# Feed-forward input products by Strassen's seven block products over token halves, with the weight sums on GpSimd

## The chip, the cores and the metric

The kernel runs on one core of a Trainium2 chip. The time is the device time of one execution in microseconds (us); the profile comes from one profiled execution and its span is counted from the first to the last instruction. The engines are named as in the profile: PE is TensorE (matmul), PEld its weight loads, DVE is VectorE, ACT is ScalarE, POOL is GpSimd, SP is the engine whose queue issues the loads.

## The reference: two decoder layers, of which the feed-forward part matters here

The program is a decoder trunk of two layers on 512 tokens of 1024 features, batch 1, all in float32. Each layer has a mixing half (a gated linear recurrence beside latent attention, merged and projected) and a feed-forward half. The change is in the second:

```
h = rms_norm(x) * (1 + sc_f) + sh_f                 # 512 x 1024
gate, up = jnp.split(h @ w_ffn_in, 2, axis=-1)      # w_ffn_in: 1024 x 5632, gate and up 512 x 2816
x = x + g_f * ((jax.nn.silu(gate) * up) @ w_ffn_out)
```

The six vectors `sh_m .. g_f` of a layer come from `c @ w_ada + b_ada`, a product of one row with a 1024 x 6144 matrix for each layer ("modulation").

## The kernel before

**Layout and precision.** Activations lie feature-major: a tile is 128 features by 512 tokens. To keep float32 accuracy every operand is split in two numbers of a type that the matmul takes at full rate (float32r): ScalarE copies the operand into the high part, VectorE subtracts it from the operand for the low part (`split`). A product takes three matmuls (`mm3`): high x high, high weights x low activations, low weights x high activations. A block of 128 output features is 8 feature tiles x 3 = 24 matmuls of 512 columns into one PSUM tile.

**Feed-forward stage.** `layer` makes `fh`, `fl` (high and low parts of the 8 tiles of h), once per layer, from x, the scale and shift columns and the broadcast `rs`, the reciprocal root of the statistics. While these are late, `Ahead.units` multiplies gate and up tile 0 with x times the scale, and the result is corrected afterwards; part of that correction runs on GpSimd. Then `gemm_units` runs over the other 21 pairs of gate and up tiles: `w_cols` loads 1024 x 128 weights (512 KB) into a `raw` buffer (three of them, `NRAW`) and splits them into `whi` and `wlo` (three of each, `NHL`); 24 matmuls; `done_fi` takes the Silu of a gate tile on ScalarE, multiplies it with the up tile on VectorE and splits the result into `ah`, `al`. The 22 activation tiles come in two halves: after tiles 0 to 10 the first half of the output product is added to the residual (8 units of 33 matmuls), after tiles 11 to 21 the second.

**Background.** After each unit `bg` issues a step of the modulation of the next layer (in layer 0's feed-forward stage, seven segments of nine steps): a load of 512 KB into `graw` (two buffers) and two VectorE operations that add it, times a column, to `macc`. `drain_bg` issues what is left before the second output product. The loads of a step are not issued before the last matmul that stood in the program at that point.

**Order.** The body only records its calls. `Recorder.order` lists them by a greedy schedule with estimated durations: each engine takes, of the calls that are ready and whose tiles have a free buffer, the one with the longest remaining path, with the matmuls chained in program order for that path. In this order each engine's queue is then written, and the engines run their queues in order. GpSimd and VectorE have durations of their own in this schedule; nothing in it lets one slow the other down. All recorded calls are issued from one line of the program, so nearly every row of the profile says L503 and is told apart by its tile names.

**Buffers.** 72 units of 128 x 512 float32 (`NU`) hold all activations and small weights; PSUM has 8 tiles of 128 x 512.

Of the kernel before, what the change touches and what calls it, by code (L numbers as in the profile page):

```python
# [13 lines left out]
F32R = mybir.dt.float32r  # L14
# [7 lines left out]
P = 128  # L22
# [3 lines left out]
KD = D // P  # L26
# [43 lines left out]
NHL = 3  # L70
# [24 lines left out]
# The body below records its engine calls in program order. order() then lists them by a  # L95
# simulated greedy schedule: each engine takes, of the calls whose operands are ready and whose
# tiles have a free buffer, the one with the longest remaining path. The calls are issued in
# that order, and Tile puts in the waits that the data needs.
# [22 lines left out]
class Ref:  # L121
    """A view of a tile that is made when the first call on it is issued."""

    def __init__(self, root, steps, dtype, part, free, off):
        self.root, self.steps, self.dtype = root, steps, dtype
        self.part, self.free, self.off = part, free, off  # (start, count), [(stride, count)], column
# [67 lines left out]
class Recorder:  # L194
# [107 lines left out]
    def order(self):  # L302
# [8 lines left out]
        # longest remaining path, with the products chained in program order  # L311
# [14 lines left out]
        # users of each tile  # L326
# [12 lines left out]
        def fits(o):  # L339
            """a free buffer for each new tile, and one more for each tile that the program makes before it"""  # L340
# [17 lines left out]
        # the clock of the tensor engine: full speed after a window full of work, half after an idle one  # L358
# [31 lines left out]
        def fill():  # L390
            """keeps the clock of the idle tensor engine up until the first products are through"""
            o = ops[self.fill] if self.fill is not None else None
            if o is None or self.fill not in issued or self.fill_end in issued or now < FILL_FROM or fills[0] >= FILL_MAX:
                return
            fills[0] += 1
            busy["PE"] = True
            res.append(o)
            heapq.heappush(events, (now + clock(now, o.dur, True), next(seq), "free", "PE"))
# [119 lines left out]
def trunk(  # L518
# [43 lines left out]
    def mm2(ps, wboth, xh, xl, start, stop):  # L562
        """high and low parts of 64 columns at once: their products lie in the two halves of the partitions"""
# [3 lines left out]
    def mm3(ps, wh, wl, xh, xl, start, stop):  # L567
        T.matmul(ps, wh, xh, start=start, stop=False)
        T.matmul(ps, wh, xl, start=False, stop=False)
        T.matmul(ps, wl, xh, start=False, stop=stop)  # L570

# [1 line left out]
    def raw_tile():  # L573
        return rec.tile(wp, [P, 1024], F32, "raw", NRAW, nm("raw"))

    def hl_tiles():
        return (
            rec.tile(wp, [P, 1024], F32R, "whi", NHL, nm("whi")),
            rec.tile(wp, [P, 1024], F32R, "wlo", NHL, nm("wlo")),
        )  # L580
# [9 lines left out]
    def w_cols(src, nk=KD, on_g=False, raws=None):  # L590
        """src: rows (k p), 128 columns; gives [(hi, lo)] over k, and adds the blocks as loaded to raws"""
# [12 lines left out]
    def w_krope(l):  # L604
        """rotary key columns: high and low parts side by side"""
# [12 lines left out]
    def w_first(l, j, keep):  # L618
        """rows of feature tile j: columns of x_lru tiles 0 and 1 and of all the down projections; gives the
        five (hi, lo), the rotary key columns' high and low parts side by side, and the columns as loaded"""  # L620
# [23 lines left out]
    def w_lru(l, n0):  # L644
        """input and recurrence gate weights of blocks n0..n0+3"""
# [8 lines left out]
    def w_rope(l, g):  # L654
        """rotary query weights of heads 4g..4g+3, as [k][half][head, 32]"""
# [16 lines left out]
    def w_pair(l, p2):  # L672
        """query (no rotary) and key/value weights of heads 2*p2, 2*p2+1"""
# [49 lines left out]
    mods = {}  # L723

    def mod_steps(l, s):
        """generator: one segment (1024 columns) of c @ w_ada[l] + b_ada[l], as columns [128, 8]"""
# [25 lines left out]
    def mod_products(l, s):  # L752
        """the same segment on the tensor engine: w_ada stationary, c moving"""
# [21 lines left out]
    # ---- work for the tensor engine while it waits at the start, so that its clock stays up  # L775
# [32 lines left out]
    def rsqrt(r, ssum, n, w, eps):  # L808
        """r = (ssum / n + EPS) ** -0.5: the reciprocal of what the Sqrt table gives, and one Newton step"""
# [11 lines left out]
    def sqrt_eps():  # L821
        """EPS as a column by the Sqrt table, not before the last call so far: the table is there
        when the statistics are"""
# [6 lines left out]
    class Stat:  # L830
# [13 lines left out]
        def finish(self, cs, n, sbuf=False):  # L844
            """rstd broadcast over partitions, in columns cs of PSUM or of a tile in SBUF"""
# [26 lines left out]
    # Across a norm the products go on before its statistics are there: the first units take x times  # L872
    # the scale, and their results are multiplied by rstd and get the shift's share as a column.
    class Ahead:
# [12 lines left out]
        def units(self, srcs):  # L887
            """products with the column blocks srcs: PSUM tiles, and the shift's columns"""
# [21 lines left out]
    def gemm_units(units, xh, xl, get_w, done):  # L910
        """units: (m, column slice); weights of m by get_w(m): list over k of (hi, lo) APs"""
# [34 lines left out]
    # The first products run by feature tile, each as soon as its modulation is there: scale and  # L946
    # shift of a few tiles at a time come from the columns of w_ada that they take.
    def first_mods(j0, nj, engs):
        """scale or shift, or both, of feature tiles j0 .. j0 + nj - 1"""
# [40 lines left out]
    def first_products(hh, hl):  # L990
# [26 lines left out]
        # Where the shift comes late, the products take the scaled tile without it, and their  # L1017
        # share of the shift is added as a column per accumulator.
# [39 lines left out]
    def tables():  # L1058
# [11 lines left out]
        # positions: rope tables and reset row  # L1070
# [16 lines left out]
        # scol = -8 softplus(-a_param), log1p(u) = 2 atanh(u / (2 + u))  # L1087
# [18 lines left out]
    def small_norm(src, gcol, n):  # L1106
        """src: list of f32 tiles; returns hi/lo tiles of rms-normed src with gain"""
# [12 lines left out]
    def layer(l, rs, ahead):  # L1120
# [13 lines left out]
        # -- down projections  # L1134
# [41 lines left out]
        # -- recurrent branch: projection, convolution, gates  # L1176
# [62 lines left out]
        # -- attention with the branch gates  # L1239
# [63 lines left out]
        def scores(h):  # L1303
            """softmax numerators and their normalisation: P[t] of [128 queries, (t + 1) * 128 keys]"""
# [23 lines left out]
        def transposes(pr):  # L1328
            """P transposed, hi and lo: per key tile, [128 keys, queries from that tile on]"""
# [36 lines left out]
        def merge(h):  # L1366
            """twice y: sigmoid(g) = (1 + tanh(g / 2)) / 2, and the half goes into the scale of the residual"""
# [18 lines left out]
        # -- output projection, residual, statistics of the next norm  # L1386
# [19 lines left out]
        # -- feed-forward  # L1406
        fh = [unit("fh", F32R) for _ in range(KD)]
        fl = [unit("fl", F32R) for _ in range(KD)]
        rs = st.finish(FULL, D, sbuf=True)
        (pg, pu), (cg, cu) = ahead.units([w_fi[l, :, c0 : c0 + P] for c0 in (0, D_FF)])  # L1410
        make_h(l, SH_F, SC_F, fh, fl, rs, FULL)
# [137 lines left out]
```

## Time and profile before

| | |
|---|---|
| median of 3 runs | 1367.09 us (1364.15 to 1371.42) |
| profiled execution, span from first to last instruction | 1361.9 us |
| busy: TensorE, VectorE, ScalarE, GpSimd | 98%, 64%, 46%, 16% |
| feed-forward stage of layer 0 | 346.67 to 700.82 us |
| feed-forward stage of layer 1 | 1000.16 to 1343.86 us |

The profiled execution's own time is its span; what lies around the span in a timed run is the 5.2 us by which the median stands above it. A timeline row has the start, the duration, the engine, and the tile written, `<-`, the tiles read; in brackets the idle time before it and what ended it. Durations of neighbours in a queue overlap by some tens of ns on VectorE and by more on TensorE, so costs in a full queue are taken from start to start.

### The profile page before, as it was taken

How to read it: one execution, taken by the hardware profiler on the slowest of the kernel's cores; microseconds unless marked ns; L12 is line 12 of the kernel's file. 1: busy time of each engine (PE TensorE's matmuls, PEld its weight loads, DVE VectorE, ACT ScalarE, POOL GpSimd, SP SyncE). 2: the span in 40 equal slices, each digit the busy share in tenths (PEclk: the TensorE clock that was granted, in tenths of full speed). 3: DMA queues.
4: the chain of work that ended last, by engine and by line, in shares of the span. 5: the costliest groups of instructions: out<-in, count | busy, mean ns of one | idle time of the engine just before them, and what ended most of it. 6: DMA issues, size and time to landing. Idle time of an engine off the chain costs nothing.

```text
span 1361.9 us, 17108 instructions
## 1 busy us (share of the span) xinstructions
PE 1339.6 (98%) x6330; PEld 1117.8 (82%) x6330; DVE 872.4 (64%) x1478; ACT 623.5 (46%) x963; POOL 213.2 (16%) x238
## 2 busy tenths in 40 slices
PE   8999989999999999999999999999999999999997
PEld 7788878887888888888888888888888888888887
DVE  5898799788856455556869887667673333333344
ACT  5585856644432222322356767855452322232223
POOL 1613334413000000000040243413400000000000
PEclk9999989999999999999999999999999999999999
DMA  9636344334655556555635333311433323433232
GB/s 300 200 96 168 103 124 140 124 117 137 194 182 164 163 159 206 178 170 184 203 86 141 92 86 100 94 47 47 124 89 98 89 75 104 120 93 95 77 88 81
DMA packets 251297, 174.92 MB, mean 128 GB/s; under 512 B 12767, under 2 KB 235341, under 8 KB 251213
## 3 DMA queue, kind: packets, MB, share of 16 engines
q1 hardware_dynamic: 251212, 173.82, 42.3%
q8 instruction: 50, 0.82, 0.2%
q14 instruction: 35, 0.28, 0.1%
HBM read 167.50 MB, written 2.10 MB: 125 GB/s over the span
## 4 chain that ended last, share of the span: by engine, by line
PE 84%; DVE 6%; DMA 5%; issue 2%; POOL 1%; ACT 1%; SPq 1%; ACTq 0%; DVEq 0%; POOLq 0%
PE mm L503 75%; PE s L503 4%; PE o L503 3%; DMA graw<-in_w_ada_dram 2%; PE pt L503 2%; DMA wa<-in_w_ada_dram 2%; DMA raw<-in_w_in_dram 1%; DVE macc L503 1%; DVE ri L503 1%; DVE wlo L503 1%; DVE xc L503 1%; POOL w L503 1%; DVE wacc L503 1%; SPq L503 1%; DVE sc L503 0%
## 5 line engine op out<-in xcount | busy, mean ns | idle before, releaser
L503 ACT ACTIVATE whi<-raw 128x1024 fp32r<-128x1024 f32 (+2 forms) x226 | 219.7, 973 | 581.3 <-PE mm L503 371.1
L503 DVE TENSOR_TENSOR wlo<-raw,whi 128x1024 fp32r<-128x1024 f32 (+2 forms) x218 | 249.3, 1145 | 205.5 <-ACT whi L503 201.2
L503 PE MATMUL mm<-fh,wlo 128*128 128x512 f32 x672 | 261.9, 390 | 0.0
L503 PE MATMUL mm<-fh,whi 128*128 128x512 f32 x672 | 261.7, 389 | 0.0
L503 PE MATMUL mm<-fl,whi 128*128 128x512 f32 x672 | 261.6, 389 | 0.0
L503 PE MATMUL mm<-hh,whi 128*128 128x512 f32 x408 | 161.3, 396 | 0.0
L503 PE MATMUL mm<-hl,whi 128*128 128x512 f32 x408 | 160.2, 393 | 0.0
L503 PE MATMUL mm<-hh,wlo 128*128 128x512 f32 x400 | 156.3, 391 | 0.0
L503 PEld LDWEIGHTS mm<-fl,whi 128*128 128x128 f32 x672 | 126.1, 188 | 26.4 <-DVE fl L503 0.2
L503 PEld LDWEIGHTS mm<-fh,wlo 128*128 128x128 f32 x672 | 126.1, 188 | 26.4 <-DVE wlo L503 0.3
L503 PEld LDWEIGHTS mm<-fh,whi 128*128 128x128 f32 x672 | 126.2, 188 | 26.0
L503 PE MATMUL mm<-ah,whi 128*128 128x512 f32 (+1 forms) x363 | 139.7, 385 | 0.0
L503 PE MATMUL mm<-ah,wlo 128*128 128x512 f32 (+1 forms) x363 | 139.3, 384 | 0.0
L503 PE MATMUL mm<-al,whi 128*128 128x512 f32 (+1 forms) x363 | 139.0, 383 | 0.0
L503 DVE SCALAR_TENSOR_TENSOR macc<-graw,cols,macc 128x512 f32<-128x512 f32 x140 | 103.8, 777 | 24.1 <-DMA graw<-in_w_ada_dram 23.7
L503 DVE TENSOR_TENSOR sg<-sg,mm 128x512 f32<-128x512 f32 x42 | 28.9, 688 | 111.1 <-PE mm L503 111.1
L503 PEld LDWEIGHTS mm<-hl,whi 128*128 128x128 f32 x408 | 77.0, 189 | 15.5 <-DVE hl L503 0.5
L503 PEld LDWEIGHTS mm<-hh,whi 128*128 128x128 f32 x408 | 77.0, 189 | 15.1 <-DVE whi L503 0.2
L503 PEld LDWEIGHTS mm<-hh,wlo 128*128 128x128 f32 x400 | 75.4, 189 | 15.8 <-POOL wlo L503 0.3
L503 PEld LDWEIGHTS mm<-ah,wlo 128*128 128x128 f32 x363 | 68.2, 188 | 13.3
L503 PEld LDWEIGHTS mm<-al,whi 128*128 128x128 f32 x363 | 68.2, 188 | 13.1
L503 PEld LDWEIGHTS mm<-ah,whi 128*128 128x128 f32 x363 | 68.2, 188 | 13.1
(266 smaller groups left out, 2173.9 us busy)
## 6 DMA issues: line engine op xcount, KB each, us to landing
raw<-in_w_ffn_in_dram SPq DMA_DIRECT2D x88, 512.0 KB, 3.9
graw<-in_w_ada_dram SPq DMA_DIRECT2D x80, 512.0 KB, 4.8
raw<-in_w_in_dram SPq DMA_DIRECT2D x49, 512.0 KB, 4.0
raw<-in_w_ffn_out_dram SPq DMA_DIRECT2D x32, 384.0 KB, 3.5
raw<-in_w_ffn_out_dram SPq DMA_DIRECT2D x32, 320.0 KB, 3.2
wa<-in_w_ada_dram SPq DMA_DIRECT2D x32, 256.0 KB, 5.6
raw<-in_w_out_dram SPq DMA_DIRECT2D x16, 512.0 KB, 3.9
raw<-in_w_uq_dram SPq DMA_DIRECT2D x24, 128.0 KB, 3.5
```

Of the source, the lines that this page charges most:

```text
L503: o.call(*(real(v) for v in o.a), **{k: real(v) for k, v in o.k.items()})
```

## The change

Each pair of a gate tile and an up tile of the 21 is now computed as a 2 x 2 block product. The block rows are gate and up, the inner blocks are features 0 to 511 and 512 to 1023, the block columns are tokens 0 to 255 and 256 to 511. Seven products of half the inner size and half the tokens take the place of eight, in the form that uses four sums of weight blocks (S1 to S4) and four of activation blocks (T1 to T4). `token_halves` makes the activation blocks once per layer, `w_quarters` the weight blocks of each pair, `fi_pair` runs the products and puts them together: three PSUM tiles of 256 columns, which take two or three products each, one after the other, and are read in between. The weight buffers `whi` and `wlo` become one kind with six buffers; a pair takes two for A1 and one for A22, and eight units for S1 to S4. Two steps of background follow each pair, as many as before. Comments are taken out elsewhere; the rest of the program is unchanged.

```diff
-NHL = 3
+NHL = 6
...
+    def w_quarters(srcs):
+        raws = []
+        for src in srcs:
+            raw = raw_tile()
+            DMA.dma_start(raw.rearrange("p (k c) -> p k c", c=P), src.rearrange("(k p) c -> p k c", p=P))
+            raws.append(raw)
+        lo_, hi_ = slice(0, 512), slice(512, 1024)
+        a11, a12, a21, a22 = raws[0][:, lo_], raws[0][:, hi_], raws[1][:, lo_], raws[1][:, hi_]
+        s1, s2, s3, s4 = (unit("ws") for _ in range(4))
+        res = {}
+        h, l_ = hl_tiles()
+        split(h, l_, raws[0])
+        res["A11"], res["A12"] = (h[:, lo_], l_[:, lo_]), (h[:, hi_], l_[:, hi_])
+
+        def add(name, s):
+            res[name] = unit("wsh", F32R), unit("wsl", F32R)
+            split(*res[name], s)
+
+        G.tensor_tensor(s1, a21, a22, ALU.add)
+        G.tensor_tensor(s2, s1, a11, ALU.subtract)
+        add("S2", s2)
+        G.tensor_tensor(s3, a11, a21, ALU.subtract)
+        add("S3", s3)
+        add("S1", s1)
+        h = hl_tile("whi")
+        split(h[:, lo_], h[:, hi_], a22)
+        res["A22"] = h[:, lo_], h[:, hi_]
+        G.tensor_tensor(s4, a12, s2, ALU.subtract)
+        add("S4", s4)
+        return res
+
+    def token_halves(first, second):
+        res = {q: [] for q in ("B11", "B21", "B22", "T1", "T2", "T3", "T4")}
+        for a, b in zip(first, second):
+            q = unit("xq", F32R)
+            split(q[:, H0], q[:, H1], a[:, H0])
+            res["B11"].append((q[:, H0], q[:, H1]))
+        t12, t34 = [], []
+        for a, b in zip(first, second):
+            t, u = unit("t12"), unit("t34")
+            V.tensor_tensor(t[:, H0], a[:, H1], a[:, H0], ALU.subtract)
+            V.tensor_tensor(t[:, H1], b[:, H1], t[:, H0], ALU.subtract)
+            G.tensor_tensor(u[:, H0], b[:, H1], a[:, H1], ALU.subtract)
+            G.tensor_tensor(u[:, H1], b[:, H0], t[:, H1], ALU.subtract)
+            t12.append(t)
+            t34.append(u)
+        for src, names in ((t12, ("T1", "T2")), (second, ("B21", "B22")), (t34, ("T3", "T4"))):
+            for t in src:
+                h, l_ = unit("xqh", F32R), unit("xql", F32R)
+                split(h, l_, t)
+                for q, cs in zip(names, (H0, H1)):
+                    res[q].append((h[:, cs], l_[:, cs]))
+        return res
...
-        make_h(l, SH_F, SC_F, fh, fl, rs, FULL)
+        ht = []
+        for j in range(KD):
+            t = unit("ht")
+            V.scalar_tensor_tensor(t, x[j], mcol(l, SC_F, j), rs, ALU.mult, ALU.mult)
+            A.activation(t, t, AF.Identity, bias=mcol(l, SH_F, j))
+            ht.append(t)
+        fx = token_halves(ht[: KD // 2], ht[KD // 2 :])
...
+        def fi_pair(fi):
+            wa = w_quarters([w_fi[l, :, c0 + fi * P : c0 + (fi + 1) * P] for c0 in (0, D_FF)])
+            a, b, z = psum("mm"), psum("mm"), psum("mm")
+            pq, u3, g, t = unit("pq"), unit("u3"), unit("sg"), unit("ut")
+            p1, u2, u3 = pq[:, H0], pq[:, H1], u3[:, H0]
+            a, b, z = a[:, H0], b[:, H0], z[:, H0]
+
+            def product(ps, w, xq, first):
+                n = len(fx[xq])
+                for k, (xh, xl) in enumerate(fx[xq]):
+                    wh, wl = (q[:, k * P : (k + 1) * P] for q in wa[w])
+                    mm3(ps, wh, wl, xh, xl, first and k == 0, k == n - 1, skip_group_check=True)
+
+            product(a, "A11", "B11", True)
+            A.activation(p1, a, AF.Copy)
+            product(b, "S2", "T2", True)
+            V.tensor_tensor(u2, b, p1, ALU.add)
+            product(a, "A12", "B21", False)
+            A.activation(g[:, H0], a, AF.Silu)
+            product(b, "S3", "T3", False)
+            V.tensor_tensor(u3, b, p1, ALU.add)
+            product(z, "S1", "T1", True)
+            V.tensor_tensor(t[:, H1], z, u3, ALU.add)
+            product(b, "A22", "T4", False)
+            V.tensor_tensor(t[:, H0], b, p1, ALU.add)
+            product(z, "S4", "B22", False)
+            V.tensor_tensor(g[:, H1], z, u2, ALU.add)
+            A.activation(g[:, H1], g[:, H1], AF.Silu)
+            V.tensor_tensor(g, g, t, ALU.mult)
+            act_split(fi, g)
+            bg(2)
...
-        gemm_units(
-            [(m, FULL) for m in range(2, 2 * NFH)], fh, fl, w_fi_cols, done_fi,
-        )
+        for fi in range(1, NFH):
+            fi_pair(fi)
```

## Rows read from the trace of the kernel before

**Rows 1.** The page: span, busy time of each engine, and the chain that ended last.
```profile
span 1361.9 us, 17108 instructions
PE 1339.6 (98%) x6330; PEld 1117.8 (82%) x6330; DVE 872.4 (64%) x1478; ACT 623.5 (46%) x963; POOL 213.2 (16%) x238
...
PE 84%; DVE 6%; DMA 5%; issue 2%; POOL 1%; ACT 1%; SPq 1%; ACTq 0%; DVEq 0%; POOLq 0%
```

**Rows 2.** Windows: length, busy us of PE, PEld, DVE, ACT, POOL, clock, DMA.
```profile
150.00:185.00 35.00, 31.74 (x155) 26.15 (x153) 29.45 (x58) 24.75 (x46) 18.65 (x18) 0.98 0.25 77
...
346.67:700.82 354.15, 354.15 (x1570) 292.51 (x1568) 221.37 (x311) 109.11 (x142) 15.27 (x22) 1.00 0.55 176
1000.16:1343.86 343.70, 343.70 (x1529) 284.53 (x1529) 130.05 (x170) 98.39 (x126) 0.00 (x0) 1.00 0.32 92
```

**Rows 3.** Groups by form, PE: count, busy us, mean ns of one.
```profile
L503 PE MATMUL mm<-fh,whi 128*128 128x512 f32 x672 | 261.7, 389 | 0.0
```

**Rows 4.** The chain in order of time: start us, length us, what.
```profile
437.56 57.24 PE mm L503 x252
...
1345.77 2.64 PE mm L503 x22
```

**Rows 5.** Timeline, DVE, from 186 us: start us, length us.
```profile
186.39 0.41 DVE L503 TENSOR_TENSOR pl<-pt,ph 128x256 fp32r<-128x256 f32 x1
186.73 0.68 DVE L503 TENSOR_TENSOR xcl<-xc,xch 128x512 fp32r<-128x512 f32 x1
187.33 0.68 DVE L503 TENSOR_TENSOR kl<-mm,kh 128x512 fp32r<-128x512 f32 x1
187.93 1.40 DVE L503 SCALAR_TENSOR_TENSOR macc<-graw,cols,macc 128x512 f32<-128x512 f32 x2
189.25 0.68 DVE L503 TENSOR_TENSOR ql<-mm,qh 128x512 fp32r<-128x512 f32 x1
```

**Rows 6.** Timeline, DVE, in layer 0's feed-forward stage.
```profile
392.35 1.23 DVE L503 TENSOR_TENSOR wlo<-raw,whi 128x1024 fp32r<-128x1024 f32 x1 [0.16 <-ACT whi L503]
393.49 0.69 DVE L503 TENSOR_TENSOR al<-sg,ah 128x512 fp32r<-128x512 f32 x1
```

**Rows 7.** Groups by form, DVE, 346.67 to 700.82 us.
```profile
L503 DVE SCALAR_TENSOR_TENSOR macc<-graw,cols,macc 128x512 f32<-128x512 f32 x98 | 69.5, 747 | 15.4 <-DMA graw<-in_w_ada_dram 15.1
...
L503 DVE TENSOR_TENSOR al<-sg,ah 128x512 fp32r<-128x512 f32 x22 | 15.1, 685 | 0.0
```

**Rows 8.** POOL: one tile's durations (ns min/median/max), and a group's mean.
```profile
L503 POOL TENSOR_TENSOR ri<-ri,sg x16: 1281/1298/2216, 176.8 to 944.9; 128x512 f32<-128x512 f32 x16
...
L503 POOL TENSOR_TENSOR wsa<-wsa 128x256 f32<-128x256 f32 x6 | 5.2, 879 | 0.2
```

**Rows 9.** Timeline, DVE and POOL, 179 to 182 us.
```profile
176.79 4.36 POOL L503 TENSOR_TENSOR ri<-ri,sg 128x512 f32<-128x512 f32 x2
178.48 1.61 DVE L503 TENSOR_TENSOR_SCAN ri<-a,ri 128x512 f32<-128x512 f32 x1
180.01 0.72 DVE L503 SCALAR_TENSOR_TENSOR xc<-mm,cols,xc 128x510 f32<-128x510 f32 x1
180.65 1.58 DVE L503 TENSOR_TENSOR wlo<-raw,whi 128x1024 fp32r<-128x1024 f32 x1
```

**Rows 10.** Timeline, DVE and POOL, from 338 us.
```profile
336.74 2.52 POOL L503 TENSOR_TENSOR wsa<-wsa,wsb 128x512 f32<-128x512 f32 x2
...
338.09 1.20 DVE L503 TENSOR_TENSOR nt<-nt,ms 128x4 f32<-128x4 f32 x1
```

**Rows 11.** Groups by form, ACT.
```profile
L503 ACT ACTIVATE whi<-raw 128x1024 fp32r<-128x1024 f32 x153 | 162.2, 1060 | 387.8 <-PE mm L503 225.3 <-issue 148.7 <-DMA raw<-in_w_in_dram 9.5
...
L503 ACT ACTIVATE ah<-sg 128x512 fp32r<-128x512 f32 x44 | 27.8, 633 | 1.9 <-DVE sg L503 0.9
```

**Rows 12.** Waits of SP's queue: us in total, times, longest us.
```profile
SPq L503 <- DVE wlo L503: 888.3, 198, 19.3
```

**Rows 13.** DMA issues: count, KB each, median us to landing.
```profile
raw<-in_w_ffn_in_dram SPq DMA_DIRECT2D x88, 512.0 KB, 3.9
```

More of the change, by code (lines that the diff above doesn't have):

```diff
@@ L565, in mm2, with mm3, hl_tile @@
         T.matmul(ps, wboth, xl, start=False, stop=stop)
[L567 to L570, printed above, removed]
+    def mm3(ps, wh, wl, xh, xl, start, stop, **k):
+        T.matmul(ps, wh, xh, start=start, stop=False, **k)
+        T.matmul(ps, wh, xl, start=False, stop=False, **k)
+        T.matmul(ps, wl, xh, start=False, stop=stop, **k)
     def raw_tile():
         return rec.tile(wp, [P, 1024], F32, "raw", NRAW, nm("raw"))
+    def hl_tile(name):
+        return rec.tile(wp, [P, 1024], F32R, "whl", NHL, nm(name))
     def hl_tiles():
-        return (
-            rec.tile(wp, [P, 1024], F32R, "whi", NHL, nm("whi")),
-            rec.tile(wp, [P, 1024], F32R, "wlo", NHL, nm("wlo")),
-        )
+        return hl_tile("whi"), hl_tile("wlo")
     def split_halves(raw, name):
@@ L1404, in layer @@
         )
-        fh = [unit("fh", F32R) for _ in range(KD)]
-        fl = [unit("fl", F32R) for _ in range(KD)]
         rs = st.finish(FULL, D, sbuf=True)
         (pg, pu), (cg, cu) = ahead.units([w_fi[l, :, c0 : c0 + P] for c0 in (0, D_FF)])
-        make_h(l, SH_F, SC_F, fh, fl, rs, FULL)
+        ht = []
[5 more added lines that the diff above has]
+        fx = token_halves(ht[: KD // 2], ht[KD // 2 :])
         if l == 0 and G_F not in EARLY_MODS:
@@ L1415, in layer, with act_split @@
             background.extend(mod_steps(l + 1, s) for s in (SC_M, SH_M, G_M, SC_F, SH_F, G_F))
-        sg, ah, al = {}, {}, {}
+        ah, al = {}, {}
+        def act_split(fi, s):
+            ah[fi], al[fi] = unit("ah", F32R), unit("al", F32R)
+            split(ah[fi], al[fi], s)
         s, t = unit("sg"), unit("ut")
@@ L1421, in layer @@
         V.scalar_tensor_tensor(s, t, cu, s, ALU.add, ALU.mult)
-        ah[0], al[0] = unit("ah", F32R), unit("al", F32R)
-        split(ah[0], al[0], s)
+        act_split(0, s)
         bg(2)
-        def done_fi(m, cs, ps):
-            fi = m // 2
-            if m % 2 == 0:
-                s = unit("sg")
-                A.activation(s[:, cs], ps[:, cs], AF.Silu)
-                sg[fi, cs.start] = s
-            else:
-                s = sg.pop((fi, cs.start))
-                V.tensor_tensor(s[:, cs], s[:, cs], ps[:, cs], ALU.mult)
-                if fi not in ah:
-                    ah[fi], al[fi] = unit("ah", F32R), unit("al", F32R)
-                split(ah[fi][:, cs], al[fi][:, cs], s[:, cs])
-        def w_fi_cols(m):
-            c0 = (m // 2) * P + (m % 2) * D_FF
-            return w_cols(w_fi[l, :, c0 : c0 + P])
+        def fi_pair(fi):
[27 more added lines that the diff above has]
+            bg(2)
         def w_fo_cols(half):
@@ L1505, in done_last @@
                         DMA.dma_start(out[0, t * P : (t + 1) * P, i * 512 : (i + 1) * 512], xo[t][i])
-        gemm_units(
-            [(m, FULL) for m in range(2, 2 * NFH)], fh, fl, w_fi_cols, done_fi,
-        )
+        for fi in range(1, NFH):
+            fi_pair(fi)
         gemm_units(
@@ L1513, in layer @@
         )
-        gemm_units([(m, FULL) for m in range(2 * NFH, 2 * NF)], fh, fl, w_fi_cols, done_fi)
+        for fi in range(NFH, NF):
+            fi_pair(fi)
         drain_bg()
```

## The prediction, made before the changed kernel was run

> **What bounds the kernel now.** I read the page's head first: TensorE is busy 98% of a span of 1361.9 us, VectorE 64%, GpSimd 16%, and the chain that ended last is 84% TensorE, 75% of it the accumulating products `mm` [rows 1]. Then the two feed-forward stretches as windows: 346.67 to 700.82 us (layer 0) and 1000.16 to 1343.86 us (layer 1). In both TensorE is busy all the time at a granted clock of 1.00, VectorE 221 of 354 us and 130 of 344 us, GpSimd 15 us and nothing [rows 2]. So these 698 us are bound by the rate of matmuls, and whatever takes columns away from TensorE is a gain as long as the helpers keep up.
>
> **Matmuls: what is removed.** A matmul's listed 389 ns [rows 3] overlaps its neighbours; the chain gives the rate: 252 products of 512 columns in 57.24 us, 0.2271 us each, and 22 products of 256 columns in 2.64 us, 0.120 us each [rows 4]. One feed-forward pair (gate and up tile) is now 2 x 8 x 3 = 48 products: 10.90 us. After, it is 7 x 4 x 3 = 84 products of 256 columns: 10.08 us. Every product keeps its own weight load; the 22 measured ones had theirs too, so its cost is inside 0.120. There are 21 such pairs in a layer (the first goes through the look-ahead unit, unchanged), 42 in all: 42 x 0.82 = 34.4 us less for TensorE, the most that the change can bring. The Trainium skill (TensorE: Matmul & The Clock Gate, Back-to-back issue gap) counts 262 cycles for 256 columns and 518 for 512; by it a pair would go from 10.4 to 9.2 us and the gain would be 50 us (estimates). The rows have both shapes, and I keep their 34.4.
>
> **VectorE: what is added.** Costs are start to start in a full queue: 256 columns 0.34 us, 512 columns 0.60, an accumulating 512 (`macc`) 0.66 [rows 5], a 1024 weight remainder 1.14 [rows 6]. Per pair before: two weight remainders, the gate product and its remainder: 2 x 1.14 + 2 x 0.60 = 3.48 us. After: one 1024 remainder (A1), four of S1 to S4 and one of A22 (512 each), four sums and one more that read PSUM (u2, u3, two of t, one of g; 256 each), g x t and its remainder: 1.14 + 5 x 0.60 + 5 x 0.34 + 2 x 0.60 = 7.04 us. In layer 0 the background modulation adds two steps per pair of two `macc` operations each: 4 x 0.66 = 2.65 us (98 accumulating ones lie in this stretch now [rows 7]).
>
> **GpSimd: four sums per pair.** A 128x512 tensor_tensor there takes 1.28 us undisturbed and up to 2.2 us [rows 8]. What else it costs stands in two stretches. At 178 us two such operations took 4.36 us instead of 2.57, while VectorE ran scans over two SBUF operands; the weight remainder that VectorE began at 180.65 ended at 182.23, 1.08 us after the GpSimd operation's end at 181.15, about its whole undisturbed time; the `xc` operation between them, which reads PSUM, took its normal 0.72 [rows 9]. At 338.09 a VectorE operation of 4 columns took 1.20 us and ended as the GpSimd operation did [rows 10]. So a GpSimd sum and a VectorE operation with two SBUF operands exclude each other for their whole length. The Trainium skill says the same (SBUF — State Buffer, Who interferes with whom): the shared ports are an exclusive lock, the second to issue blocks fully, and an operation with at most one SBUF input goes free. The trace agrees (the remainder was late by 0.50 us, `xc` not at all); by the rule the sums are not free work beside VectorE.
>
> I take 1.15 us as the hold of one sum (1.07 to 1.26 by [rows 9, 10]): 4 x 1.15 = 4.6 us per pair. Of VectorE's 7.04 us, 5.34 need the same ports; 1.70 read PSUM and can run beside a sum.
>
> **Sum per pair.** Layer 1: VectorE's stream is between 7.04 + 4.6 - 1.70 = 9.9 us (PSUM readers all under sums) and 11.6 us (none). VectorE's queue is in order, so a PSUM reader gets under a sum only if it is at the head then, about a quarter of the time: I take 0.8 us of overlap, 10.8 us. That is above TensorE's 10.08, and the two must also wait for each other. A product is 12 x 0.120 = 1.44 us, and each PSUM tile is read by VectorE between two products that accumulate into it, with one other product as cover: the read itself (0.41 us), the signals, a remainder ahead of it in the queue (0.6 to 1.14 us) and a sum's hold together exceed that often. Behind such a wait TensorE's whole queue stands, and behind VectorE's own waits the next pair's remainders. I take 11.2 us (10.08 at best; 12.5 if three of the waits cost 0.5 us each on top): (11.2 - 10.90) x 21 = +6 us, ends -17 and +34.
>
> Layer 0: the same with 2.65 us of background, which all uses the shared ports. If it stays in the pairs, 13.5 to 14.3 us; the order is made by longest remaining path, which puts background last, so some moves into the 16 output units, where VectorE has room. I take 2.3 us staying and 13.1 us: (13.1 - 10.90) x 21 = +46 us, ends -17 (all moved or hidden) and +71.
>
> **Start of the stage.** After the statistics VectorE needs 16 operations at 0.66 = 10.6 us for fh and fl [rows 5]. After: 8 scaled tiles (5.3), four 256-column remainders (1.4), eight 256-column differences (2.7) and twelve 512 remainders (7.2), 16.6 us, and eight 256-column GpSimd differences, which hold some 0.55 us each (0.88 listed [rows 8]): 21 us. The look-ahead unit covers some 6 us of that in both versions, and the products of A11 and A12 some more. As VectorE bounds what follows, little comes back: +8 us a layer (ends 0 and 10), +16.
>
> **Costed at nothing.** ScalarE: per pair 1.06 + 5 x 0.62 for weights and two conversions, 0.63 for the activation, about 1.1 for one copy and two Silus of half width: 5.9 of 10 us [rows 11]; without room it would add to the remainders' start. Bytes loaded are the same. TensorE's clock: its new waits are each shorter than the ones it now has around 150 to 185 us, where it was busy 31.74 of 35 us and the granted clock was 0.98 [rows 2]. Weight buffers are six of one kind instead of three of two.
>
> **Total.** 6 + 46 + 16 = +68 on a span of 1361.9: 1430. The median of the runs shown is 1367.09, 5.2 us above the span, which I keep: **1435 us**. With all low ends -34 (1333), with all high ends +125 (1492).
>
> **The rivals.**
> *TensorE stays the bound.* The sums find their time, waits vanish: -34 and some +10 at the starts: -24, 1343 us. For it: layer 1 leaves VectorE idle 214 of 344 us now [rows 2]. Against: in layer 0 the shared ports alone need 5.34 + 4.6 + 2.65 = 12.6 us a pair, above 10.08.
> *A split result.* Layer 1 runs at TensorE's pace (-17), layer 0 loses with most background moved out (11.6 us a pair, +15), starts +12: +10, 1377 us (1360 to 1400). It needs near-perfect packing in layer 1.
> *The weights come late.* Three raw buffers, two per pair: the second load of the next pair waits until this pair's sums have read a buffer. Loads already wait 888 us in all for a remainder to release one [rows 12]. The loop is 3.9 us to land [rows 13] + 0.4 issue + four sums at 1.28 = 9.4 us undisturbed; with half a VectorE operation ahead of each sum, over 11. SP's queue is in order, so a modulation load that waits for a late `macc` holds the weight load behind it. It decides once the loop passes 11.2 us in layer 1: 13 and 15 us a pair, +44 + 86 + 16, 1513 us.
> *The seven products don't save columns*: excluded by counting, 84 x 256 against 48 x 512.
>
> **How the numbers follow.** Shared ports as summed (1400 to 1475): 0.60. Weights late, or more waits (1475 to 1560): 0.13. Split: 0.15, of it 0.01 faster, 0.07 within 0.5% and 0.07 slower. TensorE bound: 0.12. A measurement of this kernel can tell about 0.5%, 7 us. Faster: 0.12 + 0.01 = 0.13; same: 0.07; slower: 0.60 + 0.13 + 0.07 = 0.80. The range 1360 to 1495 leaves out most of the TensorE case and the worst of the late weights; the likeliest case's own is 1400 to 1475.
>
> **What would show it.** Right: in the pairs GpSimd 128x512 operations with a mean well over 1.28 us, 512-column remainders on VectorE with a mean over 0.8 us instead of 0.685, VectorE over 90% busy in layer 0, TensorE waiting for VectorE's `u3`, `t` or remainders, a pair near 13 us in layer 0 and 11 in layer 1. Products must start 0.120 us apart inside a block. Wrong: pairs at 10.1 us in layer 1 and TensorE still 98% busy (then the sums were hidden), or TensorE waiting for `raw` loads and GpSimd more than for VectorE (then the buffers bind).

## The result: 7% slower, and where the time went

The changed kernel takes **1461.56 us** (median of 4 runs, 1460.95 to 1464.28) against 1367.4 before: a ratio of 1.070, 95% interval 1.067 to 1.072. The forecast was 1435 us; the range of 1360 to 1495 holds the measurement, and the sign is the forecast one. Its profiled execution has a span of 1459.2 us, 97.3 us more than before, and took 1460.95 us in all: what lies around a span is 1.8 us, and the rest of the 5.2 us that the forecast added was scatter between runs. Medians and ratios are of fast runs; one of the four runs of the plain start below (1494.97 us at a granted clock of 0.842) was in a slower state of the chip and is left out.

The page of the changed kernel, its head and its chain (answers to [rows 1]):

```profile
span 1459.2 us, 21243 instructions
PE 1357.9 (93%) x7842; PEld 1193.8 (82%) x7842; DVE 1164.7 (80%) x1888; ACT 737.5 (51%) x1248; POOL 501.9 (34%) x422
...
PE 57%; DVE 24%; DMA 8%; issue 6%; ACT 3%; POOL 2%; SPq 1%; ACTq 0%; DVEq 0%; POOLq 0%
```

TensorE was 84% of the chain and is 57%; VectorE went from 6% to 24%. Windows of the changed kernel: the whole feed-forward stage of layers 0 and 1 (answers to [rows 2]), then the input products of each half of the activation tiles (layer 0 first and second, layer 1 first and second). Columns as there: window, length, busy us of PE, PEld, DVE, ACT, POOL, granted clock, DMA. The two lines of layer 1's whole stage don't cover the same work: the window of before ends at 1343.86 us, and its last output product starts at 1353.19. The table below goes from product to product instead.

```profile
351.70:767.40 415.70, 364.89 (x2320) 332.58 (x2320) 371.95 (x517) 163.48 (x281) 151.85 (x109) 0.95 0.51 154
1069.23:1450.40 381.17, 355.73 (x2364) 325.66 (x2364) 274.17 (x393) 157.43 (x271) 138.73 (x87) 0.97 0.29 82
...
351.70:499.46 147.76, 118.47 (x845) 112.27 (x845) 145.49 (x195) 64.85 (x119) 64.51 (x43) 0.90 0.46 137
...
559.48:702.08 142.60, 122.65 (x930) 118.36 (x929) 138.23 (x185) 57.87 (x106) 66.28 (x40) 0.95 0.52 154
1069.23:1201.17 131.94, 114.75 (x842) 108.97 (x841) 114.16 (x159) 63.50 (x117) 65.20 (x43) 0.91 0.26 75
...
1261.15:1385.77 124.62, 116.36 (x924) 111.93 (x923) 105.07 (x138) 58.50 (x104) 67.59 (x40) 1.00 0.32 92
```

The second halves have 11 pairs and start with everything at hand: 142.60 / 11 = **12.97 us a pair in layer 0, 124.62 / 11 = 11.33 in layer 1** (10.90 before). In layer 0 VectorE is busy 97% of that time, in layer 1 84%. The first halves have 10 pairs; at these rates they would take 129.6 and 113.3 us, and they took 18.1 and 18.6 us more: the start of the stage.

| from first to last product of each kind (us) | before | changed |
|---|---|---|
| input products of layer 0, first and second half | 109.5, 120.0 | 147.8, 142.6 |
| input products of layer 1, first and second half | 108.7, 119.5 | 131.9, 124.6 |
| the four output products together, each from the last input product to its own last | 245.2 | 246.4 |

Groups by form of the changed kernel: remainders on VectorE (answers to [rows 7]; 685 ns was an undisturbed 512), a reader of PSUM, and two of the sums on GpSimd:

```profile
L503 DVE TENSOR_TENSOR wsl<-ws,wsh 128x512 fp32r<-128x512 f32 x168 | 150.9, 913 | 3.2 <-ACT wsh L503 2.9
...
L503 DVE TENSOR_TENSOR al<-sg,ah 128x512 fp32r<-128x512 f32 x44 | 42.2, 961 | 6.9 <-ACT ah L503 6.9
...
L503 DVE TENSOR_TENSOR u<-mm,pq 128x256 f32<-128x256 f32 x42 | 17.4, 414 | 3.3 <-PE mm L503 3.3
...
L503 POOL TENSOR_TENSOR ws<-raw,raw 128x512 f32<-128x512 f32 x42 | 76.7, 1826 | 0.0
...
L503 POOL TENSOR_TENSOR ws<-ws,raw 128x512 f32<-128x512 f32 x42 | 71.1, 1693 | 1.4 <-POOL ws L503 0.5
```

Both sides lengthen each other: the 512 remainder from 0.685 to 0.913 or 0.961 us, the GpSimd sum from 1.28 to 1.7 or 1.8. The reader of PSUM stays at its 0.41. The timeline of layer 1's second half shows how (VectorE and GpSimd rows; start, length, engine):

```profile
1281.93 2.26 POOL L503 TENSOR_TENSOR ws<-raw,raw 128x512 f32<-128x512 f32 x1
1283.31 1.43 DVE L503 TENSOR_TENSOR wsl<-ws,wsh 128x512 fp32r<-128x512 f32 x1
1284.16 1.74 POOL L503 TENSOR_TENSOR ws<-ws,raw 128x512 f32<-128x512 f32 x1
1284.67 0.41 DVE L503 TENSOR_TENSOR ut<-mm,u 128x256 f32<-128x256 f32 x1
1285.00 1.44 DVE L503 TENSOR_TENSOR wsl<-ws,wsh 128x512 fp32r<-128x512 f32 x1
1285.97 1.63 POOL L503 TENSOR_TENSOR ws<-raw,ws 128x512 f32<-128x512 f32 x1
1286.36 0.41 DVE L503 TENSOR_TENSOR ut<-mm,pq 128x256 f32<-128x256 f32 x1
1286.70 1.45 DVE L503 TENSOR_TENSOR whi<-raw,whi 128x512 fp32r<-128x512 f32 x1
```

The sums end at 1284.19, 1285.90 and 1287.60; the three remainders, begun 0.88 to 0.90 us before these ends, end at 1284.74, 1286.44 and 1288.15, each 0.54 or 0.55 us after them: nearly a whole remainder's time comes behind the sum. Both `ut`, which read PSUM, run in 0.41 us beside a sum.

### The profile page after: what moved, and what is told of

Read it like the earlier page. It is cut to its first block, busy times and chain, and to the rows that moved or that the text cites. A ratio compares the mean times of both kernels' runs of the same rounds, so it can differ in the third digit from the quotient of the medians.

```text
span 1459.2 us, 21243 instructions
## 1 busy us (share of the span) xinstructions
PE 1357.9 (93%) x7842; PEld 1193.8 (82%) x7842; DVE 1164.7 (80%) x1888; ACT 737.5 (51%) x1248; POOL 501.9 (34%) x422
## 4 chain that ended last, share of the span: by engine, by line
PE 57%; DVE 24%; DMA 8%; issue 6%; ACT 3%; POOL 2%; SPq 1%; ACTq 0%; DVEq 0%; POOLq 0%
PE mm L503 48%; PE s L503 4%; DVE wsl L503 4%; DVE wlo L503 3%; DVE macc L503 3%; DMA raw<-in_w_ffn_in_dram 3%; PE o L503 2%; DMA graw<-in_w_ada_dram 2%; PE pt L503 2%; DVE whi L503 2%; DVE ht L503 1%; DVE xql L503 1%; ACT whi L503 1%; DMA raw<-in_w_in_dram 1%; POOL ws L503 1%
## 5 line engine op out<-in xcount | busy, mean ns | idle before, releaser
L503 PE MATMUL mm<-xqh,wsh 128*128 128x256 f32 x672 | 200.9, 299 | 21.8 <-DVE pq L503 14.9
L503 PE MATMUL mm<-xql,wsh 128*128 128x256 f32 x672 | 197.7, 295 | 4.5 <-DVE xql L503 4.5
L503 PE MATMUL mm<-xqh,wsl 128*128 128x256 f32 x672 | 195.9, 292 | 2.2 <-DVE wsl L503 2.0
L503 PEld LDWEIGHTS mm<-xqh,wsh 128*128 128x128 f32 x672 | 135.5, 202 | 28.8 <-DVE pq L503 18.0
L503 PE MATMUL mm<-xqh,whi 128*128 128x256 f32 x504 | 122.9, 299 | 36.1 <-DVE u L503 22.2
L503 DVE TENSOR_TENSOR wsl<-ws,wsh 128x512 fp32r<-128x512 f32 x168 | 150.9, 913 | 3.2 <-ACT wsh L503 2.9
L503 PEld LDWEIGHTS mm<-xql,wsh 128*128 128x128 f32 x672 | 135.5, 202 | 6.9 <-DVE xql L503 6.7
L503 PEld LDWEIGHTS mm<-xqh,wsl 128*128 128x128 f32 x672 | 134.9, 201 | 3.2 <-DVE wsl L503 3.2
L503 ACT ACTIVATE wsh<-ws 128x512 fp32r<-128x512 f32 x168 | 101.4, 623 | 64.1 <-POOL ws L503 63.2
L503 PE MATMUL mm<-xql,whi 128*128 128x256 f32 x336 | 97.7, 291 | 0.0
```

Source lines behind the costliest of these rows:

```text
L503: o.call(*(real(v) for v in o.a), **{k: real(v) for k, v in o.k.items()})
```

## The experiments

Each is compared with the kernel before, timed on the same chip. The question of the first two: do the sums cost what they cost because they run on GpSimd?

**Sums on VectorE.** The same for s2, s3, s4:

```diff
-        G.tensor_tensor(s1, a21, a22, ALU.add)
+        V.tensor_tensor(s1, a21, a22, ALU.add)
...
```

> The four weight sums per pair move from GpSimd to VectorE; nothing else changes. Theory (the sums on GpSimd shut VectorE out for their whole length): VectorE gets 4 x 0.60 = 2.4 us more work per pair and loses 3.8 us of waiting. Steady pairs of layer 1 go from 11.34 to 10.3-10.8 us, those of layer 0 from 13.0 to 11.7-12.2 us, the first halves lose 4 us each: some 45-55 us faster than the changed kernel, 1405-1420 us, and 512-column remainders on VectorE go back to a mean of 0.68-0.72 us. Rival (VectorE is full by its own instruction count and the sums on GpSimd are work taken off it): 42 x 2.4 = 100 us slower, near 1560 us.

Measured: 1406.99 us, ratio 1.029 (1.025 to 1.032): 55 us better by giving VectorE *more* to do. **No sums** (left out, plain weight blocks multiplied in their place):

```diff
-        add("S2", s2)
+        add("S2", a11)
...
```

> The four weight sums are left out: raw weight blocks stand in their place, with the same splits and products; the output is not the reference's. Theory: VectorE's 7.04 us per pair now run without waits, so layer 1's pairs are bound by TensorE at 10.1-10.4 us and layer 0's (7.04 + 2.3 to 2.65 of background) at 10.1-10.6 us; with 5-10 us less at each start, 1360-1380 us. Rival (the reads of PSUM between accumulating products set the pair, not the sums): layer 1's pairs stay near 11.3 us and the time above 1410 us.

Measured: 1364.59 us, ratio 0.999 (0.997 to 1.000). Second halves of both layers, with sums on VectorE, then without sums:

```profile
554.15:685.30 131.15, 117.62 (x930) 114.99 (x928) 124.62 (x216) 57.38 (x104) 0.00 (x0) 0.97 0.56 168
1226.20:1336.95 110.75, 110.75 (x924) 110.75 (x923) 101.03 (x178) 56.16 (x104) 0.00 (x0) 1.00 0.36 102
```

```profile
536.26:647.83 111.57, 111.57 (x928) 111.28 (x927) 103.12 (x184) 53.77 (x100) 0.00 (x0) 1.00 0.61 191
1182.43:1293.28 110.85, 110.85 (x924) 110.79 (x923) 78.38 (x136) 54.93 (x102) 0.00 (x0) 1.00 0.35 101
```

In layer 1 both run at 10.07 us a pair: 110.75 us for 924 products, 0.120 us each, the promised rate, with TensorE never idle. In layer 0 with the sums on VectorE, VectorE is busy 95% of the half, which takes 11.92 us a pair, near VectorE's own 9.44 + 2.65 = 12.1 (with sums and background).

This leaves a rival: splits and products might wait for GpSimd's slow chain, or for the raw buffers that it holds. **Unread sums** and **a fourth raw buffer** tell them apart. In the variant without sums:

```diff
         res["A11"], res["A12"] = (h[:, lo_], l_[:, lo_]), (h[:, hi_], l_[:, hi_])
+        for i in range(4):
+            G.tensor_tensor(unit("ws"), f(h[:, lo_]), x[i], ALU.add)
...
```

> The variant without weight sums (it multiplies plain weight blocks in their place, so it leaves the sums out) with four GpSimd additions per pair of the same shape added, whose results nothing reads and which read no raw buffer (they read the high part of A1 and the residual). So no dependence and no buffer hangs on GpSimd; only its use of memory stays. Theory (the sums cost by holding the ports that VectorE shares): 4 x 1.15 = 4.6 us of hold come back, weight remainders of 512 columns at 0.85 us or more instead of 0.68, 1425 to 1460 us. Rival (the sums cost because splits and products wait for GpSimd's slow chain and for the raw buffers that it holds): 1362 to 1375 us and remainders near 0.7 us.

Measured: 1465.13 us, ratio 1.073 (1.070 to 1.075). Nothing reads these sums and they read no raw buffer, and the time is the changed kernel's again. They do read the high part of A1, but nothing waits long for that: the one wait for GpSimd's `ws` in this run is 1.2 us. One row tells it, the 512 remainder without sums and with unread ones:

```profile
L503 DVE TENSOR_TENSOR wsl<-raw,wsh 128x512 fp32r<-128x512 f32 x168 | 111.3, 683 | 10.0 <-ACT wsh L503 9.9
```

```profile
L503 DVE TENSOR_TENSOR wsl<-raw,wsh 128x512 fp32r<-128x512 f32 x168 | 168.2, 1021 | 5.0 <-ACT wsh L503 4.8
```

**Two unread sums** (`range(2)`) ask what one costs:

> The variant without weight sums (they are left out) with two unread GpSimd additions per pair instead of four. If a sum costs VectorE its hold, and time is lost only once VectorE's pair passes TensorE's 10.08 us: with 1.08 us a sum (from layer 1 at four: 11.38 - 7.04, by four), layer 1's pair needs 7.04 + 2.16 = 9.2 us of VectorE and stays at 10.1 to 10.2 us; layer 0's needs 11.5 to 11.9 and takes that. 1365 + 21 x 1.5 + some 3 = 1398 us (1385 to 1410). If each addition instead costs the kernel a fixed amount, half of the 100 us between none and four: 1415 us, with layer 1's second half near 118 us.

Measured: 1398.17 us, ratio 1.023 (1.020 to 1.027). The second halves of layers 0 and 1:

```profile
540.12:663.10 122.98, 114.84 (x929) 112.00 (x927) 119.21 (x188) 54.87 (x102) 33.98 (x19) 1.00 0.56 174
1208.44:1321.06 112.62, 111.65 (x924) 110.94 (x923) 86.55 (x136) 54.15 (x102) 37.10 (x19) 1.00 0.35 101
```

Against no sums, layer 1 loses 1.8 us on this half and layer 0, where VectorE was busy 92% without sums, loses 11.4. Two sums are nearly free where VectorE has room. A full VectorE is not the condition, though: four cost layer 1's half 13.8 us (124.62 - 110.85) with VectorE busy 84%. VectorE's busy time rises by 0.4 us a sum in layer 1 (86.55 - 78.38 over 22) and 0.7 in layer 0, not by the 1.08 of the expectation. That its total came out is partly luck: with the first halves layer 0 loses 20.8 us instead of 31.5, and layer 1 loses 9.2 where some 3 us for all the rest were expected.

**A fourth raw buffer**:

```diff
-NU = 72
-NRAW = 3
+NU = 70
+NRAW = 4
```

> The changed kernel with four raw weight buffers instead of three (and 70 units instead of 72, for the room). Theory A, after the run that moved the background work and gained nothing: the loop load, GpSimd sums, release of a raw buffer is a second bound of layer 0, where loads land in 5 to 6.7 us instead of 3.9. Then layer 0's pairs fall from 12.97 us to about 11.7, 21 x 1.2 = 25 us: 1430 to 1442 us. Rival B, VectorE together with the sums' hold of the shared ports is the only bound: within 8 us of 1461, 1453 to 1469, and GpSimd's wait for raw loads shrinks without a gain in time.

Measured: 1488.56 us, ratio 1.090 (1.087 to 1.093), outside both. Of the 27 us more, 14 had passed before the first pair (366.1 us instead of 351.7; two units fewer also change the order there). The halves took 152.0, 144.5, 138.0 and 124.7 us: none gained, so theory A's 25 us did not come. The run also takes two units away, which may hide a smaller gain; that the loss is the units' was not tried. The unread sums, which hold no raw buffer and cost as much, are the stronger sign that raw buffers don't bind.

Now the background in layer 0. **Background moved** (one step a pair, three a unit in the first output product):

```diff
-            bg(2)
+            if fi >= NFH or (l, G_F) not in mods:
+                bg(1)
...
```

> Background of the next layer's modulation: in layer 0 one step per pair instead of two (none once its first segment is done in the first half), three per unit instead of one in the first output product, the rest before the second. Theory (layer 0 differs from layer 1 by the background on the shared ports): layer 0's pairs go from 13.0 us to 11.4-12.1 us, the output units stay at 7.5 us, layer 1 is unchanged: 20-33 us faster, 1428-1442 us. Rival (layer 0 is slow for its loads or its start): within 10 us of the changed kernel.

Measured: 1470.41 us, ratio 1.076 (1.073 to 1.080): a miss for the theory, within the 10 us of the rival. VectorE's busy time in layer 0's second half fell from 138.23 to 127.21 us and the half from 142.6 only to 141.5; the first output product grew from 59.8 to 66.3 us.

**Background's additions cut** to 16 of 512 columns, loads kept:

```diff
+                    if l == 1 or s == G_F:
+                        hs = slice(h * 512, h * 512 + 16)
```

> The changed kernel with the background's loads of layer 0's feed-forward stage kept as they are, but 7 of every 8 steps add only 16 of each 512 columns (so most of the modulation sums of that stage are left out). Theory (layer 0's pairs take 12.97 us and layer 1's 11.33 because the background's accumulations fill VectorE): layer 0's pairs fall to 11.3 to 11.9 us, its halves from 147.8 and 142.6 us to about 133 and 127; 1425 to 1440 us. Rival, left by the two runs that moved background work and added a buffer without a gain (the background's loads slow the weights' loads): nothing changes by more than 10 us, 1451 to 1471.

Measured: 1448.34 us, ratio 1.059 (1.057 to 1.061), between the two: halves of layer 0 at 142.7 and 131.2 us. VectorE's rows that write or read `macc` in layer 0's second half, in the changed kernel and in this one (the column after the length is their busy time):

```profile
559.48:702.08 142.60, 45.21 (x42) 0.95 0.52 154
```

```profile
557.30:688.45 131.15, 24.83 (x40) 0.97 0.53 166
```

The cut takes away less than half of these rows' time: 34 operations of 16 columns, which take 0.22 to 1.37 us each, and six others are left. **No background at all**:

```diff
-            background.append(mod_steps(0, G_F))
+            mods[0, G_F] = mods[0, G_M]
...
```

(and layer 1's six likewise)

> The changed kernel with no background at all in layer 0's feed-forward stage, neither loads nor accumulations (the modulation columns of layer 0's mixing half are used in place of those it would make, so that part of the computation is left out). With the loads kept and nearly all accumulations left out, layer 0's halves were 142.7 and 131.2 us where layer 1's are 132 and 125. Theory (the background's loads hold up the weights' loads, and that is what remains): both halves fall to layer 1's, about 133 and 125 us, and the whole to 1425 to 1434 us. Rival (something else of layer 0 keeps it): halves near 142 and 131, 1438 to 1450 us.

Measured: 1421.25 us, ratio 1.039 (1.036 to 1.043), a little under the range. Second halves of layers 0 and 1:

```profile
539.69:663.21 123.52, 116.57 (x924) 111.92 (x923) 103.72 (x138) 58.50 (x104) 68.84 (x40) 1.00 0.32 92
1219.93:1345.09 125.16, 116.89 (x924) 113.25 (x923) 102.73 (x138) 58.18 (x104) 66.88 (x40) 0.99 0.31 91
```

With first halves of 132.0 and 131.7 us the layers are now equal. So background makes all of layer 0's excess over layer 1: 16.5 us of its two halves went with the cut of the additions (147.8 - 142.7 and 142.6 - 131.2), 18.4 us are the rest of it: its loads and the operations left on VectorE. What of this the loads are stays open: a weight load's median landing in layer 0's second half is 4.6 us in the changed kernel, 4.1 with the additions cut and 3.7 without background, and SP's queue waits there 23.4, 15.4 and 0 us for `macc`; no run took these apart.

Last the start. **Filled start**: 45 useless products of 256 columns ahead of each of two block products of pair 1, to keep the clock up:

```diff
+            if fi == 1:
+                warm(45)
             product(a, "A11", "B11", True)
```

> 90 matmuls without use (256 columns, 16-bit) are put on TensorE at the start of each feed-forward stage, while it waits for the first activation blocks. In the changed kernel the granted clock is at its half level for 17 us from 367 and from 1084 us. Theory A (that stretch is paced by VectorE, so the clock costs nothing there): the half level goes away or gets shorter and the time stays within 6 us of the changed kernel, or rises by up to 10 us. Theory B (the half clock is what made the start cost 18 us a layer instead of 8): 12-20 us faster.

Measured: 1461.33 us, ratio 1.069 (1.066 to 1.072): no gain. But the filling did not take the half level away. The stretches at the half level (a granted clock of 0.50, 1.2 GHz) at the starts of layers 0 and 1, in the changed kernel and then in the filled one:

```profile
356.00:373.10 17.10, 11.67 (x41) 9.02 (x40) 17.10 (x22) 12.70 (x24) 10.04 (x8) 0.50 0.00 1
1072.80:1089.90 17.10, 12.29 (x44) 9.94 (x45) 17.10 (x25) 13.62 (x24) 9.33 (x8) 0.50 0.00 0
```

```profile
364.80:381.90 17.10, 10.53 (x42) 9.35 (x43) 15.59 (x23) 5.73 (x9) 4.41 (x4) 0.50 0.30 87
1081.60:1091.80 10.20, 6.78 (x28) 6.23 (x29) 9.45 (x15) 4.55 (x7) 1.29 (x1) 0.50 0.00 0
```

In the changed kernel they begin at 356.0 and 1072.8 us, 11 us before the times in the expectation. With the filling (348 to 359 and 1067 to 1078 us) the stretch of layer 0 comes 8.8 us later and is as long, and that of layer 1 is 6.9 us shorter; layer 1's first half takes 126.1 us instead of 131.9 but starts 2.5 us later. So this run doesn't settle what the half level costs. What speaks for theory A is the first pair of lines: VectorE is busy 17.10 of 17.10 us in both, and TensorE only 11.67 and 12.29, so VectorE set the pace there. That is argued from rows, not shown by a run.

**Plain start**: the changed kernel with tiles and products of pairs 1 to 3 as before, token sums made meanwhile (their other products read halves of `fh`, `fl`):

```diff
-            fi_pair(fi)
+            (fi_pair if strassen(fi) else fi_plain)(fi)      # strassen: fi >= 4
...
```

> The changed kernel, GpSimd sums and background as they are, but in both layers the activation tiles and their products for pairs 1 to 3 are made as in the kernel before; the token sums follow while these run, and Strassen begins with pair 4. Theory (each layer loses some 18 us at the start of the stage, because VectorE makes block tiles, token sums and weight remainders beside GpSimd's sums before TensorE has work): the start loss goes, 2 x 18 us, and three plain pairs save 3 x 2.1 us in layer 0 and 3 x 0.4 us in layer 1; layer 0 keeps a few us, as VectorE has token sums and background there: 1415 to 1432 us, first halves near 129 us and 114 us instead of 147.8 and 131.9. Rival (the first halves are long because all their pairs are slow): only the plain pairs gain, 1450 to 1460 us.

Measured: 1420.96 us (three runs), ratio 1.040 (1.037 to 1.042). First halves 127.3 and 116.1 us, 20.5 and 15.9 us less. Of these 36.4 us some 7.5 are the three plain pairs' (3 x 2.1 and 3 x 0.4), the other 29 are the start: most of its 36.7.

**A mixed version.** The seven products only where VectorE has room, pair by pair, all sums (the token sums too) on VectorE:

```diff
...
+            return fi >= 3 if last else fi >= 4 and fi % 2 == 0
...
```

> A version that takes the seven products only where VectorE has room: all sums on VectorE, the plain products and their activation tiles kept for the first two pairs of layer 1 and for pairs 1 to 3 and every odd pair of layer 0, Strassen for the other 19 and 9 pairs; background one step with a Strassen pair and three with a plain one. By the pairs measured with the sums on VectorE (10.07 us against 10.90) it gains 28 x 0.83 = 23 us, less a few us for waits where the kinds meet: 1345 us (1338 to 1356), about 1.6% under the kernel before. Rival (the token sums and the mixed pairs disturb the start or the order as they did in the changed kernel): 1362 us or more.

Measured: 1356.82 us, ratio 0.993 (0.991 to 0.995): 0.7% faster than before, less than summed and just outside the range. Layer 0's first half took 117.1 us. Hence the next, with `fi > NFH and fi % 2 == 0` in layer 0:

> The mixed version with Strassen pairs of layer 0 only in the second half of its activation tiles (every second one of 12 to 20), so that the token sums and the three background steps per plain pair don't fall into the start of the stage; background in the first half two steps a pair as in the kernel before. In the first mixed version the first half of layer 0 took 117.1 us where 4 x 10.07 + 6 x 10.90 = 105.7 was expected, the other three halves came out as summed. Theory (VectorE was overfilled there by token sums plus background): the first half returns to about 109.7 us as in the kernel before, 7.4 us less than the first mixed version: 1349 us (1344 to 1354). Rival (keeping two forms of the activations costs that time itself, through units or ScalarE): 1354 us or more.

Measured: **1350.1 us, ratio 0.987 (0.985 to 0.990)**, in the range: 1.3% faster than the kernel before. Layer 0's halves, then layer 1's second:

```profile
350.64:460.17 109.53, 109.53 (x486) 90.26 (x485) 79.63 (x122) 42.95 (x59) 0.00 (x0) 1.00 0.54 174
520.50:636.49 115.99, 115.99 (x713) 104.66 (x711) 96.26 (x156) 45.99 (x73) 0.00 (x0) 1.00 0.60 185
1164.23:1274.98 110.75, 110.75 (x925) 110.75 (x923) 101.11 (x178) 56.62 (x104) 0.00 (x0) 1.00 0.36 102
```

TensorE is busy to the last us in all three: 24 pairs at 10.07 instead of 10.90 us give 19.9 us, and 17.5 arrive.

## Why the prediction was right, and which term was too small

**The sign and the mechanism** were right and are shown, not only argued: the sums hold what VectorE needs. The hold was read from two stretches of the kernel before [rows 9, 10]; sums that nobody reads cost 100.5 us (1465.13 against 1364.59), the real ones 97.0. The Trainium skill (SBUF — State Buffer, Who interferes with whom) has it as a rule, an exclusive lock on the shared ports alone; the timeline above agrees, with 0.54 to 0.55 us after each sum's end and 0.41 us beside one.

**The signs named** came: GpSimd's sums at 1.49 to 1.83 us, 512 remainders at 0.91 us, VectorE at 97% in layer 0. TensorE's waits in the changed kernel (us in total, times, longest):

```profile
PE mm L503 <- DVE u L503: 22.2, 16, 3.5
...
PE mm L503 <- DVE pq L503: 14.9, 10, 3.1
PE mm L503 <- ACT pq L503: 13.2, 13, 2.5
...
PE mm L503 <- DVE xq L503: 9.8, 7, 3.8
```

They are the forecast waits for a read of a PSUM tile between two products (by ScalarE too, which makes the first read), and (`xq`) for the start.

**The sum, term by term**, on the span (forecast +68, measured +97.3):

| term | forecast | measured |
|---|---|---|
| layer 1, 21 pairs | 11.2 us: +6 | 11.33 us: 21 x 0.43 = +9.0 |
| layer 0, 21 pairs | 13.1 us: +46 | 12.97 us: 21 x 2.07 = +43.5 |
| start of the stage, both layers | 2 x 8 = +16 | 18.1 + 18.6 = +36.7 |
| before layer 0's first pair (351.70 against 347.03) | none | +4.7 |
| output products | none | +1.2 |
| between the two stages | none | +2.2 |

No run traced the 4.7 and the 2.2 us. **The step that failed in size is the start**, "+8 us a layer (ends 0 and 10)": even its upper end was about half of what came. In layer 0, after the statistics, the changed kernel and then the kernel before:

```profile
344.00:374.00 30.00, 20.63 (x81) 16.25 (x80) 29.85 (x36) 21.68 (x39) 19.72 (x17) 0.69 0.15 53
```

```profile
340.00:370.00 30.00, 29.98 (x135) 24.49 (x136) 26.73 (x39) 15.96 (x21) 1.47 (x3) 1.00 0.57 176
```

The kernel before keeps TensorE busy for 29.98 of these 30 us although VectorE makes `fh` and `fl` in them. The forecast's 8 us, at most 10, are about the difference of its 21 us and those 10.6, as if the 10.6 had cost time before. In the changed kernel VectorE is busy all the time, and TensorE waits. The 21 us were right where no weight sums run. The first and last rows of VectorE's work on the tiles of layer 0, in the changed kernel and without weight sums:

```profile
344.15 9.38 DVE L503 SCALAR_TENSOR_TENSOR ht<-x,mod,rs 128x512 f32<-128x512 f32 x8 [1.84 <-ACT rs L503]
...
371.96 1.88 DVE L503 TENSOR_TENSOR xql<-t,xqh 128x512 fp32r<-128x512 f32 x3
```

```profile
349.38 6.61 DVE L503 SCALAR_TENSOR_TENSOR ht<-x,mod,rs 128x512 f32<-128x512 f32 x8 [0.77 <-ACT rs L503]
...
368.89 1.88 DVE L503 TENSOR_TENSOR xql<-t,xqh 128x512 fp32r<-128x512 f32 x3
```

That is 29.7 us with the weight sums and 21.4 without: the forecast did not count that the eight weight sums of the first two pairs run beside the tiles (341 to 367.5 us on GpSimd). They are not the bulk of the start, however. Without any weight sums the first halves take 121.6 and 112.2 us where 10 pairs at that variant's rates are 101.4 and 100.8: 31.6 us too long in all. With the sums on VectorE the same reckoning gives 34.4 (136.0 and 118.3 against 119.2 and 100.7), in the changed kernel 36.7. So most of the start comes with the block tiles and token sums themselves, whoever makes the weight sums, and it nearly uses up the 34.4 us that the seven products save. That is why the variant without sums only equals the kernel before, and why a plain start is worth so much.

**Where a right number had a partly wrong working.** In layer 0 the 2.07 us a pair were forecast as background that fills VectorE. The layers differ by 1.64 us a pair, less than the 2.3 taken for the background. The cut of its additions gives back 1.03 of them (142.6 - 131.2 over 11); the other 0.6 are its remaining operations and perhaps its loads, "costed at nothing" as unchanged bytes. Layer 1's 11.33 is not a full VectorE either (84%): it is the waits in both directions, which the forecast priced by choice at 0.4 us over VectorE's 10.8. VectorE's rows there hold only 105.07 / 11 = 9.55 us, since a sum lengthened them by 0.6 us (105.07 - 78.38 over 44) and not by the 0.95 left of 1.15 after overlap; the waits are thus larger, 1.8 us a pair. That the two errors cancel, and the pair comes within 0.13 us of the forecast, is luck.

**The rivals.** Late weights: GpSimd did wait for raw loads, but a fourth buffer gained nothing, and sums that read no raw buffer cost as much. TensorE as the bound: in the second halves it is what remains once GpSimd is idle, in layer 1 with the sums on VectorE and in both layers without sums. The clock, costed at nothing because the new waits were to be short, did fall to its half level for 17.1 us in each start; VectorE had no idle time there, but no run isolated what it cost.

## What to carry to other kernels

An idle GpSimd is not free help for a VectorE that works on two SBUF operands: with the additions moved there VectorE was busier than when it did them itself (105.07 against 101.03 us in layer 1's second half, 138.23 against 124.62 in layer 0's), and moving them back was worth 55 us. Before trading matmuls for sums, count the stage's start as a stage of its own, with everything that must be ready before its products, and compare VectorE's time for a pair with TensorE's. Where a trade pays only with room on another engine, apply it pair by pair where the windows show that room.

## What the hardware showed that was not expected

GpSimd's additions are held up as well: 1.28 us undisturbed, 1.49 to 1.83 in the pairs. The price of a sum is not fixed: two a pair cost layer 1's half 1.8 us and four 13.8, with VectorE busy 77% and 84%. And useless products ahead of a stage's start did not keep the granted clock up: the half level came 8.8 us later and lasted as long in layer 0 (17.1 us), 10.2 instead of 17.1 us in layer 1.
